# A float32 result tile for VectorE's top-k counts in a streaming hybrid encoder step

## The chip, the cores and the metric

The kernel runs on one core of one Trainium2 chip. The metric is the device time of one execution in microseconds. Three runs of the kernel before took 1585.16, 1585.86 and 1586.07 us; the median is 1585.86 us.

## The reference

One layer of an encoder works on 1024 new prompt frames and on 8 running streams of 16 frames, 1152 rows in all, each of 1024 features. After an RMSNorm a projection feeds two groups of heads side by side: a gated linear recurrence (the LRU: convolution over 4 frames, two gates, a scan) and sparse attention. An output projection and a SwiGLU feed-forward (2816 wide) with residuals close the layer. The part that matters here is how the attention chooses its keys:

```python
idx_score = einsum('bths,bth->bts', relu(sc), wi)          # one score per query and key
idx_score = where(adm, idx_score, -inf)                    # chunk-causal
vals, sel = lax.top_k(idx_score, topk)                     # 256 keys (prompt), 132 (streams)
```

For each query only the 256 (132) best keys take part in the softmax. The kernel doesn't sort: it finds each query's threshold bit by bit, and turns the scores into a mask of zeros and large negative numbers.

## The kernel before, in words

The rows are nine tiles of 128 queries: tiles 0 to 7 are the prompt, tile 8 (`NP`) the streams. Tiles 0 and 1 need no choice. The stages run after one another, with overlap: norm and the key and value projection, index scores, the LRU, the q projection, half of the output projection, attention, the other half, the feed-forward. All large products are matrix multiplications in three passes on split float32 (`mm3`; each pass is issued at line 205).

The threshold search runs in two groups (`TK`, read in `topk`). The group of tiles 2 to 5 counts on ScalarE: `activation(..., Sign, accum_out=cnt)`, 32 rounds of four counts. The group of tiles 6, 7 and 8 counts on VectorE: 16 rounds on the high 16 bits of the scores, a step (`topk_lower`) that makes a 16-bit key of what is left, and 16 more rounds, with three counts to a round (896, 1024 and 528 elements wide). A count is a `tensor_scalar` with `is_ge` whose elementwise result nobody reads; only the sum in `accum_out` is used. The result went to `jk[0]`, a bfloat16 tile that later stages use as well: `topk_lower` for a temporary, `topk_mask` for its equality mask, `sample_prep` for a copy of the last mask. After each round two or three tiny VectorE instructions (3 or 4 elements wide) update the candidate threshold (`cand`, `t`), for both groups: a ScalarE count of the next round waits for VectorE too.

Two planners set the order of the work. The first is the kernel's own: `run` steps generators (streams of work and `side` work) along an estimated clock, and `Metered` prices each instruction as it is issued. A VectorE instruction with `accum_out` and a 16-bit input is priced at 0.07 us plus half of 0.00104 us an element; the input's type decides, the result's type isn't looked at. That planner fixes the order in which the program is written down. The second is the scheduler of `TileContext(nc, schedule_with_timeline_sim=True)`: from the written order as priority, the dependencies and its own estimate of each instruction's time it sets the order in which each engine's queue finally holds its instructions. Within `step`, the top-k's instructions get a priority 400 places later than where they are written (`LATER`), so that they give way to others and fill gaps:

```python
    LATER = {'vector': 400, 'scalar': 400}
        with self.tc.high_priority(offset=-n):
            return next(g, None)
```

On the chip each engine's queue then runs strictly in that order. Instructions of one engine that the profile names by line 66 are all those recorded by `Metered`, so the tiles tell them apart: `jk` and `key` are the counts, `tk_cand` and `tk_cnt` the candidate updates, `xp`, `xc`, `tr`, `ti`, `tt` the LRU, `qn` and `rp` the queries, `acc` the output projection.

The LRU stage (`lru_main`): the matrix products of a third go to PSUM, ScalarE copies them out (`xp`), TensorE does the convolution on the copy (line 210), ScalarE adds the bias (`xc`), TensorE does the two gates, ScalarE and VectorE the rest.

Of the kernel before, what the change touches and what calls it, by code (L numbers as in the profile page):

```python
# [9 lines left out]
F32 = mybir.dt.float32  # L10
# [71 lines left out]
class Kernel:  # L82
# [181 lines left out]
    def build(self, upto=99):  # L264
        ctx, tc, nc, I, O = self.ctx, self.tc, self.nc, self.I, self.O
# [34 lines left out]
        with tc.tile_pool(name="t1a", bufs=2, side=R) as tp:  # L300
            g, wk = self.load_kv_weights(tp)
# [4 lines left out]
        groups = self.groups = [self.tk_group(n, t, a) for n, (t, a) in enumerate(self.TK)]  # L306
        widest = [max([2] + [s.shape[1] for i, s in self.s.items() for n, b in self.TK if i in n and a == b]) for a in range(2)]
        self.jk = [(tka_p if a else self.tk_p).tile([128, widest[a]], BF16, name=f"jk{a}") for a in range(2)]
        self.scored, self.masked, self.tk_done = set(), {0, 1}, set()
        self.qst, self.qst_t = {}, {}  # L310
        self.n_lru, self.spare = 0, None
# [531 lines left out]
    def topk_count(self, g, t, less=False):  # L843

        nc = self.nc
        for j, i in enumerate(g["tiles"]):
            w = self.s[i].shape[1]
            if g["act"]:
                nc.scalar.activation(self.jk[1][:, :w], self.s[i], AF.Sign, bias=t[:, j:j + 1],
                                     accum_out=g["cnt"][:, j:j + 1])  # L850
                continue
            k = 132 if i == NP else 256
            nc.vector.tensor_scalar(self.jk[0][:, :w], g["keys"][j], t[:, j:j + 1], 0.5 - k if less else None,
                                    op0=ALU.is_ge, op1=ALU.add, accum_out=g["cnt"][:, j:j + 1])
            if j % 2 and j + 1 < g["n"]:
                yield 0.0
# [893 lines left out]
```

## Time and profile before

| what | value |
|---|---|
| three runs, median | 1585.86 us |
| the profiled execution, its own time | 1582.82 us |
| its span in the profile | 1580.7 us |
| TensorE clock granted, mean | 0.969 |
| VectorE, ScalarE, GpSimd instructions | 1909, 1484, 433 |

The profile is of one execution. Its span is the time from the first to the last recorded instruction; the 2.1 us around it are in the execution's own time. Busy time of an engine is the time in which it works on an instruction; it doesn't count the time in which its queue's first instruction waits. An arrow `x <- y` between engines reads "waited for", one between tiles "written from".

### The profile page before, as it was taken

To read this page: it belongs to the slowest core of one execution; us is meant where nothing else is said; L and a number is where in the kernel's file an instruction comes from. 1 tells how busy PE (TensorE), PEld (TensorE's weight loads), DVE (VectorE), ACT (ScalarE), POOL (GpSimd) and SP (SyncE) were. 2 spreads that over 40 slices of the span, in tenths; PEclk is the share of its full clock that TensorE was granted. 3 is DMA by queue.
4 is the path that set the end of the run, shared out by engine and by line. 5 is a ranking of instruction groups with operands and counts; after the bars stand their busy time and mean duration, and the time that the engine had idled before them with its cause. 6 is when DMAs were issued, how large, how long until landed. Compare 5 with 4: busy or idle time off the path is not lost.

```text
span 1580.7 us, 21030 instructions
## 1 busy us (share of the span) xinstructions
PE 1477.3 (93%) x7858; PEld 1335.3 (84%) x7858; DVE 886.4 (56%) x1909; ACT 624.4 (39%) x1484; POOL 288.7 (18%) x433
## 2 busy tenths in 40 slices
PE   6899898875989899999999999999999999999998
PEld 6777676764977688888999999999898989898987
DVE  7656899998676887768424242423333242424143
ACT  5447967867631987755312120202020202121100
POOL 5424223227484444400000000000000000000000
PEclk7999899988999899999999999999999999999999
DMA  7211110100140001120302020202020202111002
GB/s 241 66 32 42 35 29 16 29 14 14 44 156 0 8 14 47 48 67 28 94 14 67 14 75 6 80 1 80 1 80 0 81 18 63 30 51 52 29 1 120
DMA packets 93798, 74.66 MB, mean 47 GB/s; under 512 B 13236, under 2 KB 84532, under 8 KB 93696
## 3 DMA queue, kind: packets, MB, share of 16 engines
q1 hardware_dynamic: 93696, 73.32, 15.5%
q8 instruction: 62, 1.02, 0.3%
q14 instruction: 40, 0.33, 0.1%
HBM read 67.03 MB, written 6.27 MB: 46 GB/s over the span
## 4 chain that ended last, share of the span: by engine, by line
PE 72%; DVE 15%; ACT 5%; POOL 3%; issue 3%; DMA 1%; SPq 0%; POOLq 0%; ACTq 0%; DVEq 0%
PE ps L205 67%; DVE jk L66 7%; PE ps L215 3%; DVE tk_cand L66 2%; ACT jk L66 1%; DVE tr L66 1%; POOL rp L66 1%; PE ps L210 1%; DVE ti L66 1%; POOL qn L66 1%; DVE s L66 1%; ACT qeo L66 1%; ACT m L66 1%; ACT relu L66 0%; DMA tab<-in_rope_dram 0%
## 5 line engine op out<-in xcount | busy, mean ns | idle before, releaser
L205 PE MATMUL ps<-hf,w 128*128 128x384 f32 x2556 | 460.6, 338 | 0.0
L205 PEld LDWEIGHTS ps<-hf,w 128*128 128x128 f32 x2556 | 451.5, 187 | 0.8
L205 PE MATMUL ps<-w,a 128*128 128x512 f32 x999 | 239.1, 390 | 0.0
L66 DVE TENSOR_TENSOR acc<-ps,acc 128x512 f32<-128x512 f32 x234 | 161.3, 690 | 134.4 <-PE ps L205 133.9
L205 PEld LDWEIGHTS ps<-w,a 128*128 128x128 f32 x999 | 187.3, 188 | 40.1
L66 ACT ACTIVATE w<-raw 128x512 fp32r<-128x512 f32 x128 | 77.8, 630 | 303.0 <-PE ps L205 220.9
L66 DVE TENSOR_TENSOR sg<-ps,sg 128x384 f32<-128x384 f32 x66 | 36.7, 557 | 276.4 <-PE ps L205 275.9
L66 DVE TENSOR_TENSOR w<-raw,w 128x512 fp32r<-128x512 f32 x116 | 76.8, 687 | 87.4 <-ACT w L66 87.2
L66 ACT ACTIVATE jk<-s,tk_cand 128x384 bf16<-128x384 f32 (+3 forms) x128 | 99.4, 776 | 61.8 <-DVE tk_cand L66 53.0
L66 ACT ACTIVATE a<-sg 128x384 fp32r<-128x384 f32 x66 | 34.5, 523 | 217.9 <-DVE sg L66 217.9
L205 PE MATMUL ps<-hf,rest 128*128 128x384 f32 x612 | 114.5, 334 | 0.0
L205 PE MATMUL ps<-h,w 128*128 128x384 f32 x576 | 108.7, 347 | 0.5 <-ACT relu L66 0.5
L205 PEld LDWEIGHTS ps<-hf,rest 128*128 128x128 f32 x612 | 106.9, 188 | 0.2
L205 PEld LDWEIGHTS ps<-h,w 128*128 128x128 f32 x576 | 102.3, 190 | 4.7 <-ACT relu L66 0.6
L205 PE MATMUL ps<-w,h 128*128 128x256 f32 (+1 forms) x600 | 94.6, 314 | 0.6 <-DVE to L66 0.6
L205 PE MATMUL ps<-w,rest 128*128 128x512 f32 x324 | 83.0, 406 | 8.2 <-POOL rest L66 8.0
L205 PEld LDWEIGHTS ps<-w,h 128*128 128x128 f32 x600 | 82.2, 188 | 7.3 <-DVE to L66 0.9
L205 PEld LDWEIGHTS ps<-w,rest 128*128 128x128 f32 x324 | 61.3, 194 | 22.7 <-POOL rest L66 8.9
L66 ACT ACTIVATE sg<-ps 128x384 f32<-128x384 f32 x66 | 32.1, 486 | 122.0 <-PE ps L205 122.0
L210 PE MATMUL ps<-xp,taps 128*128 128x384 f32 (+2 forms) x128 | 44.5, 504 | 37.7 <-ACT xp L66 37.7
L210 PEld LDWEIGHTS ps<-xp,taps 128*128 128x128 f32 x128 | 26.7, 231 | 51.7 <-issue 43.8
L66 POOL TENSOR_SCALAR m<-m,mx 128x128 f32<-128x128 f32 (+7 forms) x64 | 47.6, 752 | 68.5 <-DVE mx L66 61.7
(261 smaller groups left out, 2185.2 us busy)
## 6 DMA issues: line engine op xcount, KB each, us to landing
raw<-in_w_ffn_in_dram SPq DMA_DIRECT2D x44, 512.0 KB, 4.9
raw<-in_w_ffn_out_dram SPq DMA_DIRECT2D x22, 512.0 KB, 3.5
raw<-in_w_in_dram SPq DMA_DIRECT2D x16, 512.0 KB, 3.8
out_dram<-acc SPq DMA_DIRECT2D x9, 512.0 KB, 2.6
x<-in_x_prompt_dram SPq DMA_DIRECT2D x8, 512.0 KB
acc<-in_x_prompt_dram SPq DMA_DIRECT2D x8, 512.0 KB, 9.1
tab<-in_rope_dram SPq DMA_DIRECT2D x34, 64.0 KB, 1.8
raw<-in_w_out_dram SPq DMA_DIRECT2D x4, 512.0 KB, 3.5
```

Of the source, the lines that this page charges most:

```text
L66: return f(*args, **kw)
L205: self.nc.tensor.matmul(out, lhsT, rhs, start=start, stop=stop)
L210: self.nc.tensor.matmul(out, lhsT, rhs, start=start, stop=stop)
L215: self.nc.tensor.transpose(out, in_, self.ident[0:n, 0:n])
```

## The change

The counts of the VectorE group write their unused elementwise result to a tile of their own, `junk`, of float32, 1024 wide. `jk[0]` stays for its other uses. Nothing else is edited: the inputs, the operation, the sum and the number of instructions are the same. The new tile takes 4 KB of each partition.

```diff
         self.jk = [(tka_p if a else self.tk_p).tile([128, widest[a]], BF16, name=f"jk{a}") for a in range(2)]
+        self.junk = self.tk_p.tile([128, widest[0]], F32, name="junk")
 ...
             k = 132 if i == NP else 256
-            nc.vector.tensor_scalar(self.jk[0][:, :w], g["keys"][j], t[:, j:j + 1], 0.5 - k if less else None,
+            nc.vector.tensor_scalar(self.junk[:, :w], g["keys"][j], t[:, j:j + 1], 0.5 - k if less else None,
                                     op0=ALU.is_ge, op1=ALU.add, accum_out=g["cnt"][:, j:j + 1])
```

## Rows read from the trace of the kernel before

**Rows 1.** First part of the page: busy time, share, instructions of each engine.
```profile
PE 1477.3 (93%) x7858; PEld 1335.3 (84%) x7858; DVE 886.4 (56%) x1909; ACT 624.4 (39%) x1484; POOL 288.7 (18%) x433
```
**Rows 2.** Busy time by stretch; columns: from:to, length, engines, clock, DMA share, GB/s.
```profile
180.00:262.00 82.00, 74.27 (x358) 64.88 (x357) 79.05 (x233) 64.62 (x143) 15.22 (x26) 0.94 0.09 22
180.00:412.00 232.00, 185.18 (x913) 159.04 (x912) 216.14 (x534) 168.63 (x354) 72.23 (x96) 0.92 0.07 20
412.00:500.00 88.00, 79.00 (x476) 69.74 (x475) 60.95 (x107) 33.86 (x193) 65.54 (x82) 0.94 0.27 90
500.00:560.00 60.00, 52.50 (x280) 43.88 (x279) 47.16 (x163) 45.94 (x123) 21.92 (x40) 0.91 0.02 5
700.00:1000.00 300.00, 299.84 (x1586) 278.69 (x1585) 132.95 (x239) 76.54 (x144) 0.00 (x0) 1.00 0.14 42
1000.00:1580.00 580.00, 576.28 (x3016) 540.47 (x3014) 201.79 (x319) 93.40 (x174) 0.00 (x0) 1.00 0.15 47
```
**Rows 3.** Waits of PE, then ACT, 180 to 412 us: total us, times, longest.
```profile
PE ps L210 <- ACT xp L66: 37.7, 9, 8.9
PE ps L210 <- ACT xc L66: 8.6, 3, 3.8
...
ACT jk L66 <- DVE tk_cand L66: 48.3, 18, 5.6
```
**Rows 4.** Timeline of PE, 262 to 412 us: start, length, what, [idle before].
```profile
294.48 1.56 PE L210 MATMUL ps<-xc,bd 128*128 128x384 f32 x4 [3.84 <-ACT xc L66]
...
340.57 3.52 PE L210 MATMUL ps<-xp,taps 128*128 128x256 f32 x8 [8.91 <-ACT xp L66]
370.77 4.64 PE L210 MATMUL ps<-xp,taps 128*128 128x384 f32 x8 [8.08 <-ACT xp L66]
388.64 3.38 PE L210 MATMUL ps<-xp,taps 128*128 128x256 f32 x8 [7.77 <-ACT xp L66]
```
**Rows 5.** Timeline of ACT around those waits of PE.
```profile
338.60 0.61 ACT L66 ACTIVATE jk<-s,tk_cand 128x384 bf16<-128x384 f32 x1 [2.45 <-DVE tk_cand L66]
...
340.06 0.53 ACT L66 ACTIVATE xp<-ps 128x256 f32<-128x256 f32 x2
...
363.25 0.61 ACT L66 ACTIVATE jk<-s,tk_cand 128x384 bf16<-128x384 f32 x1
...
370.15 0.47 ACT L66 ACTIVATE xp<-ps 128x384 f32<-128x384 f32 x1
...
386.67 0.61 ACT L66 ACTIVATE jk<-s,tk_cand 128x384 bf16<-128x384 f32 x1 [5.61 <-DVE tk_cand L66]
```
**Rows 6.** Timeline of DVE, 330 to 339 us.
```profile
330.89 1.15 DVE L66 TENSOR_SCALAR_CACHE_REDUCE jk<-key,tk_cnt 128x896 bf16<-128x896 int16 x1
...
334.61 1.15 DVE L66 TENSOR_SCALAR_CACHE_REDUCE jk<-key,tk_cnt 128x896 bf16<-128x896 int16 x1
...
338.16 0.16 DVE L66 SCALAR_TENSOR_TENSOR tk_cand<-tk_cnt 128x4 int32<-128x4 f32 x1
```
**Rows 7.** Costliest DVE groups by form, 180 to 412 us: busy us, mean ns.
```profile
L66 DVE TENSOR_SCALAR_CACHE_REDUCE jk<-key,tk_cand 128x1024 bf16<-128x1024 bf16 x16 | 20.4, 1276 | 0.2
L66 DVE TENSOR_SCALAR_CACHE_REDUCE jk<-key,tk_cand 128x896 bf16<-128x896 bf16 x16 | 18.2, 1138 | 0.0
L66 DVE TENSOR_SCALAR_CACHE_REDUCE jk<-key,tk_cand 128x528 bf16<-128x528 bf16 x16 | 12.2, 761 | 0.2
L66 DVE TENSOR_SCALAR_CACHE_REDUCE jk<-key,tk_cnt 128x1024 bf16<-128x1024 int16 x16 | 20.5, 1278 | 0.4
L66 DVE DVE_READ_ACCUMULATOR jk<-key,tk_cand 128x1 f32 x48 | 3.9, 82 | 0.0
L66 DVE TENSOR_SCALAR jk<-jk,tk_cand,tk_cnt 128x512 f32<-128x512 f32 x4 | 2.2, 538 | 0.1
L66 DVE TENSOR_SCALAR key<-jk 128x512 int16<-128x512 f32 x4 | 1.7, 420 | 0.1
```
**Rows 8.** Timeline of DVE: a sum that writes float32, and first use of a mask.
```profile
371.17 1.25 DVE L66 TENSOR_SCALAR_CACHE_REDUCE s<-s,tk_cnt 128x1024 f32<-128x1024 f32 x1
...
534.03 0.55 DVE L66 CUSTOM_DVE_ANT_0 m<-ps,s 128x384 f32<-128x384 f32 x1
```
**Rows 9.** Timeline of POOL: the first mask of ScalarE's group is finished.
```profile
462.50 0.57 POOL L66 TENSOR_SCALAR s<-s 128x384 f32<-128x384 f32 x1
```
**Rows 10.** Timeline of PE: first use of what follows the VectorE group's masks.
```profile
587.19 0.27 PE L205 MATMUL ps<-jk,key 128*128 128x264 bf16 x1
```
**Rows 11.** Timeline of DVE: the copy of the last mask.
```profile
392.72 0.43 DVE L66 CAST jk<-s 128x528 bf16<-128x528 f32 x1 [0.53 <-POOL s L66]
```

## Prediction

> **What bounds the kernel now.** I read the page's first part, then busy time by stretch, then the waits of the stretches that are not full. TensorE is busy 93% of the span [rows 1]. By stretch it is full from 700 us to the end (299.84 of 300, then 576.28 of 580), and nothing on VectorE can matter there. The holes lie earlier: in 180 to 412 us, the LRU stage and all 96 counts of VectorE, TensorE works 185.18 of 232 us, so 46.8 us are idle [rows 2]. The waits name the cause of nearly all of it: 37.7 us for ScalarE's copy `xp` and 8.6 us for `xc`, 46.3 us together [rows 3].
>
> Why is the copy late? The timelines show a queue blocked at its head. At 340.57 TensorE has been idle for 8.91 us; the copy it needs starts at 340.06, behind a ScalarE count that had itself waited 2.45 us, to 338.60, for a candidate update on VectorE [rows 4, 5]. That update runs at 338.16, behind VectorE's counts, which follow each other from 330.89 on [rows 6]. At 388.64 it is the same: 7.77 us of idle TensorE, a count that waited 5.61 us [rows 4, 5]. In 180 to 412 ScalarE stood still 48.3 us on such updates, 18 times, with LRU copies queued behind [rows 3]. VectorE is the full engine of that stretch: 216.14 of 232 us [rows 2]. So the stage is paced by VectorE, through ScalarE's order, and TensorE pays.
>
> The sizes say what the scheduler may have got wrong. A round of three counts takes 1.276 + 1.138 + 0.761 us and three accumulator reads of 0.082, 3.42 us [rows 7]; one round's first count starts 3.72 us after the last one's (330.89 to 334.61) [rows 6]. The kernel's own meter prices the three at 3 x 0.07 + 2448 x 0.00052 = 1.48 us. A planner that believes that puts a ScalarE count early in ScalarE's queue, sure that its candidate will be there, and ahead of LRU copies; on the chip the candidate isn't there.
>
> **The change part by part.**
>
> *The duration of the 96 counts.* No row has this form with a 16-bit input and a float32 result. The nearest is the sum that reads and writes float32: 1.25 us at 1024 elements, against 1.276 for the count now [rows 7, 8]. That is below by 0.026 us: 96 x 0.026 = 2.5 us of VectorE less at the most. From above, the only rows in which a wider result goes with a longer time are two plain operations of the same width, 0.538 us to float32 and 0.420 us to int16 [rows 7]: a ratio of 1.28, though they differ in their scalar operands too. On the counts' busy time, that of the three groups with the 16-bit float key and as much again for the three with the integer key (whose 1024-wide group has 20.5 us against 20.4), 2 x (20.4 + 18.2 + 12.2) = 101.6 us [rows 7], that would be +28 us. I take 0, since the row with a sum is the nearest by far; the 28 us stay as a rival.
>
> The Trainium skill ("VectorE: DVE Perf Modes", section on the perf-mode tier table) speaks against the change here: it puts `tensor_scalar` at 4x for bfloat16 in SBUF and 2x for float32, so a wider result would drop the counts a tier. The plain operations' rows fit its 2x (0.538 us for 512 elements), the counts don't fit its 4x: 1024 elements in 1.276 us is less than one element a cycle at the page's 0.96 GHz. By the page as it stands the counts would get slower; by the row there is no faster mode to lose. The trace doesn't bear the page out for counts.
>
> *The extra tile.* It takes room, no instruction and no wait. The counts share their result tile with nobody else now; but all users of `jk[0]` around the counts are on VectorE too, one queue, so no wait goes: 0.
>
> *The kernel's own planner.* It prices by the input's type, which stays 16-bit. The written order and the due times don't move: 0.
>
> *The scheduler's order.* This is the whole effect. Its price for a count isn't in the profile, before or after. From both sides: nothing (it priced them alike) up to all of the 46.3 us of TensorE's waits [rows 3]; and a loss, below. To choose, I assume that it prices as the meter would: half rate for 16-bit throughout, full rate once a float32 is in it. A round is then believed to take 3 x 0.07 + 2448 x 0.00104 = 2.76 us instead of 1.48, against 3.42 on the chip: the error falls from 1.94 to 0.66 us a round, by 66%. A scheduler that sees VectorE busy sees the candidates come late, and puts ScalarE's LRU copies ahead of the counts that wait for them. 0.66 x 46.3 = 31 us. Not all of that can come: at 370.77 TensorE's 8.08 us were lost though the count at 363.25 hadn't waited for a candidate at all; the copy was behind four counts' own work and other LRU instructions [rows 4, 5]. I take off a third and keep 20 us.
>
> *What is late next.* VectorE's work doesn't shrink. In a stage shortened to 212 us, at the 96% that VectorE reached at its densest (79.05 of 82 us, 180 to 262) [rows 2], it does 204 of its 216 us; 12 us move behind the LRU, to 412 to 500, where VectorE has 88 - 60.95 = 27 us idle [rows 2] but also carries the query rotation and the output projection's sums. I charge half, 6 us. The masks have room: the VectorE group's last mask is copied at 392.72 and first used at 587.19 [rows 10, 11], 194 us; the first mask of ScalarE's group is ready at 463.07 and used at 534.03 [rows 8, 9], 71 us. If that cover is gone each further microsecond costs one.
>
> *Sum.* 1582.8 (the profiled execution) + 0 + 0 - 20 + 6 = 1568.8 us. The runs' median is 3.0 us above the profiled execution (1585.86 against 1582.82), so I say 1572 us.
>
> **The rivals.**
>
> *1. The order changes and the time doesn't.* For: VectorE is 93% busy in the stage whatever the order, so a copy freed early may meet an LRU instruction held on VectorE. Or the scheduler priced both forms alike, and the queues stay as they are. Against: ScalarE's 48.3 us of standing still are head-of-queue waits, and such waits depend on order alone. Time: 1583 to 1589.
>
> *2. The counts go too late (slower).* If the scheduler now holds VectorE's counts back behind everything it can find, rounds land after 412 us, in front of VectorE's sums and query work, which TensorE and GpSimd need. A round is 3.72 us; behind 412 there are 27 us idle to 500 and 12.8 to 560 [rows 2, 6], 40 in all. It decides from the point where the rounds moved exceed the idle time plus the gain: (40 + 20)/3.72, 16 of 32 rounds. At 19 rounds: 71 - 40 - 20 = +11, so about 1597. For: the top-k's instructions rank 400 places back, and every believed microsecond more makes them lose more contests. Against: they rank as far back now, and fill what is idle; the stage offers few other instructions to VectorE.
>
> *3. The chip pays for the wider result.* +28 us on an engine that paces its stage, of which the better order may give back some: 28 - 14 = +14, 1600. Against it stands the row with a sum into float32.
>
> **How the numbers follow.** A run can tell about 0.2% (3.2 us) from no change. Forecast (faster, own range 1555 to 1582): 0.60. Rival 1: 0.14. Rival 2: 0.22. Rival 3: 0.04. So faster 0.60, same 0.14, slower 0.26. The range must leave out no more than 2 in 10. The low end takes most of the order's 46.3 us with little given back: 1585.9 - 36 = 1550, about 5% left out below. The high end takes in rival 2 to its 19 rounds, 1597, and leaves out its worse half and most of rival 3: about 13%.
>
> **What would show it.** Right: counts of 1.28 us at 1024 in the profile after; in the LRU stage fewer waits of ScalarE's counts for `tk_cand` (48 us now) and of TensorE for `xp` (38 us now), the last LRU convolution earlier than 388 us by 15 to 20 us, and part of VectorE's counts or masks after it. The stages from attention on start earlier by about 14 us and have the same length. Wrong: counts near 1.6 us (rival 3); the same waits at the same places (rival 1); waits of TensorE for VectorE's `acc` or of GpSimd for `qn` in the 100 us after the LRU, or attention's first masked score waiting for a mask (rival 2).

## The result and the profile after

The kernel after takes 1565.93 us (median of 4 runs, 1565.71 to 1566.31) against 1585.96 us for the kernel before on the same chip: a ratio of 0.9877, 95% interval 0.9861 to 0.9892. The profiled execution took 1565.71 us, its span is 1563.9 us.

The first part of its page, beside [rows 1]:

```profile
PE 1472.8 (94%) x7858; PEld 1332.3 (85%) x7858; DVE 887.8 (57%) x1909; ACT 624.8 (40%) x1484; POOL 290.1 (19%) x433
```

Same instructions, nearly the same busy time on every engine. TensorE's busy time fell by 4.5 us, the span by 16.8: what went is mostly idle time of TensorE. To find where, I cut both traces at the start of the LRU's last convolutions on `xp` (393.14 us before, 362.53 after) and at the matrix product that first uses the VectorE group's masks [rows 10], which now starts at 571.39 us. Busy time by stretch (columns as in rows 2), the kernel before and then after:

```profile
0.00:180.00 180.00, 149.95 (x759) 126.67 (x760) 121.58 (x266) 107.28 (x268) 76.55 (x156) 0.91 0.30 88
180.00:393.14 213.14, 167.58 (x772) 142.16 (x771) 204.29 (x505) 156.05 (x331) 68.98 (x90) 0.91 0.08 22
393.14:587.19 194.05, 175.37 (x1048) 152.90 (x1047) 142.74 (x367) 113.97 (x383) 100.46 (x138) 0.95 0.13 44
587.19:1580.70 993.51, 984.44 (x5283) 913.59 (x5282) 417.80 (x774) 247.06 (x505) 42.68 (x50) 1.00 0.15 46
```
```profile
0.00:180.00 180.00, 149.03 (x750) 125.85 (x751) 120.61 (x262) 105.41 (x263) 76.14 (x156) 0.91 0.30 88
180.00:362.53 182.53, 162.92 (x780) 140.84 (x780) 168.18 (x447) 154.67 (x328) 56.00 (x84) 0.94 0.09 25
362.53:571.39 208.86, 177.78 (x1048) 153.25 (x1047) 181.10 (x427) 117.81 (x392) 115.37 (x144) 0.93 0.12 41
571.39:1563.90 992.51, 983.10 (x5283) 912.30 (x5282) 417.87 (x774) 246.91 (x505) 42.57 (x50) 1.00 0.15 46
```

The LRU stage is 30.6 us shorter, the stretch behind it 14.8 us longer, the rest 1.0 us shorter: together 16.8. Of the 30.6 us, 26.0 are idle time of TensorE (45.6 to 19.6), and 4.7 are busy time, at a mean granted clock of 0.94 instead of 0.91; of the 14.8 us, 12.4 are idle time (18.7 to 31.1). The fifth figure of each row (VectorE's busy time) says how: VectorE does 36.1 us less ahead of the LRU's end (204.29 to 168.18) and 38.4 us more behind it (142.74 to 181.10). ScalarE's work ahead of it hardly changes (156.05 to 154.67). Work of VectorE was put off, and the LRU went past it.

The waits that answer to [rows 3], the kernel after, TensorE and then ScalarE, 180 to 412 us:

```profile
PE ps L210 <- ACT xp L66: 18.4, 5, 5.7
...
PE ps L210 <- ACT xc L66: 0.7, 1, 0.7
```
```profile
ACT jk L66 <- DVE tk_cand L66: 21.0, 10, 4.6
```

TensorE's waits for the two copies fall from 46.3 us to 19.1, ScalarE's for the candidate from 48.3 to 21.0. The counts themselves, by form (busy us, mean ns), beside [rows 7]:

```profile
L66 DVE TENSOR_SCALAR_CACHE_REDUCE junk<-key,tk_cnt 128x1024 f32<-128x1024 int16 x16 | 20.4, 1274 | 0.1
L66 DVE TENSOR_SCALAR_CACHE_REDUCE junk<-key,tk_cand 128x1024 f32<-128x1024 bf16 x16 | 20.4, 1274 | 0.2
L66 DVE TENSOR_SCALAR_CACHE_REDUCE junk<-key,tk_cnt 128x896 f32<-128x896 int16 x16 | 18.2, 1140 | 0.3
...
L66 DVE TENSOR_SCALAR_CACHE_REDUCE junk<-key,tk_cand 128x528 f32<-128x528 bf16 x16 | 12.1, 756 | 0.0
```

1274 ns against 1276 for 1024 elements: the wider result costs nothing.

What was put off is best seen at the LRU's scans on VectorE. The LRU runs in four passes; the first scan of each pass, before and then after (timelines of VectorE; start, length):

```profile
265.04 0.95 DVE L66 TENSOR_TENSOR_SCAN tr<-tt,ti 128x384 f32<-128x384 f32 x1
...
317.99 0.95 DVE L66 TENSOR_TENSOR_SCAN tr<-tt,ti 128x384 f32<-128x384 f32 x1
...
374.12 0.94 DVE L66 TENSOR_TENSOR_SCAN tr<-tt,ti 128x384 f32<-128x384 f32 x1
...
409.45 0.95 DVE L66 TENSOR_TENSOR_SCAN tr<-tt,ti 128x384 f32<-128x384 f32 x1
```
```profile
255.54 0.95 DVE L66 TENSOR_TENSOR_SCAN tr<-tt,ti 128x384 f32<-128x384 f32 x1
...
297.93 0.95 DVE L66 TENSOR_TENSOR_SCAN tr<-tt,ti 128x384 f32<-128x384 f32 x1
...
340.23 0.95 DVE L66 TENSOR_TENSOR_SCAN tr<-tt,ti 128x384 f32<-128x384 f32 x1
...
378.48 0.95 DVE L66 TENSOR_TENSOR_SCAN tr<-tt,ti 128x384 f32<-128x384 f32 x1
```

From scan to scan the passes took 53.0, 56.1 and 35.3 us; now 42.4, 42.3 and 38.3. Counting along each engine's queue gives the reason (an engine runs its queue strictly in order, as the forced orders below show too, so this needs no times):

```
                                                      pass 1   2    3    4
VectorE counts ahead of the pass's first scan, before     48   72   96   96   (of 96)
                                               after      36   50   72   90
ScalarE counts ahead of the pass's last xp copy, before   48   72   98  118   (of 128)
                                                 after    48   68   92  113
```

In VectorE's queue the LRU overtakes 12, 22, 24 and 6 counts. At the 3.42 us of a round of three that is 13.7, 25.1, 27.4 and 6.8 us of VectorE's work that no longer stands ahead of the scans. In ScalarE's queue only up to six counts change sides. The last count now starts at 398.26 us (352.70 before), and the three scans that build VectorE's masks, which ran from 355.02 to 384.33, now run from 405.35 to 433.33.

### The profile page after: what moved, and what is told of

It is laid out like the page before. It is cut to its first block, busy times and chain, and to the rows that moved or that the text cites. A ratio compares the mean times of both kernels' runs of the same rounds, so it can differ in the third digit from the quotient of the medians.

```text
span 1563.9 us, 21015 instructions
## 1 busy us (share of the span) xinstructions
PE 1472.8 (94%) x7858; PEld 1332.3 (85%) x7858; DVE 887.8 (57%) x1909; ACT 624.8 (40%) x1484; POOL 290.1 (19%) x433
## 4 chain that ended last, share of the span: by engine, by line
PE 74%; DVE 10%; ACT 9%; issue 3%; POOL 3%; DMA 1%; SPq 0%; POOLq 0%; ACTq 0%; DVEq 0%
PE ps L205 69%; ACT jk L66 4%; PE ps L215 4%; DVE junk L66 2%; PE ps L210 1%; DVE tk_cand L66 1%; ACT L66 1%; POOL rp L66 1%; DVE tr L66 1%; DVE jk L66 1%; DVE ti L66 1%; ACT qeo L66 1%; ACT tr L66 1%; DVE qn L66 1%; DVE s L66 1%
## 5 line engine op out<-in xcount | busy, mean ns | idle before, releaser
L66 ACT ACTIVATE jk<-s,tk_cand 128x384 bf16<-128x384 f32 (+3 forms) x128 | 99.4, 777 | 31.3 <-DVE tk_cand L66 25.8
L210 PE MATMUL ps<-xp,taps 128*128 128x384 f32 (+2 forms) x128 | 40.1, 466 | 19.1 <-ACT xp L66 18.4
L205 PE MATMUL ps<-smr,vhl 128*128 128x512 f32 x162 | 53.8, 418 | 2.7 <-ACT smr L66 2.7
```

The costliest lines, as they stand in the source:

```text
L66: return f(*args, **kw)
L205: self.nc.tensor.matmul(out, lhsT, rhs, start=start, stop=stop)
L210: self.nc.tensor.matmul(out, lhsT, rhs, start=start, stop=stop)
```

## The experiments

Ratios are to the kernel before on the same chip, with 95% intervals. Where nothing else is said, waits are TensorE's for `xp` and `xc` in 180 to 412 us.

**Room or type.** The first run keeps bfloat16 in a tile of its own; the second has the float32 result but lets the tile double as `jk[0]`, so it has no room of its own.

```diff
-        self.junk = self.tk_p.tile([128, widest[0]], F32, name="junk")         # first run
+        self.junk = self.tk_p.tile([128, 2 * widest[0]], BF16, name="junk")   # first run
 ...
+        self.jk[0] = self.junk.bitcast(BF16)                                  # second run, with the F32 tile
```

> The counts get room of their own, 4 KB of a partition as in the change, but the result stays bfloat16. Theory (the scheduler's longer estimate of a float32 result makes the order): as before, 1583 to 1589 us, with about 46 us of TensorE's waits for xp and xc in the LRU stage; the queues do differ a little, since the first count after topk_lower no longer has to follow its temporaries in jk[0]. Rival (the own room takes away a dependency, and that is what pays): 1563 to 1570 us, waits for xp and xc near 19 us.

> No room of its own: the counts write a float32 tile that also serves as jk[0] for topk_lower, the masks and the mask copy. Theory (estimate): 1563 to 1572 us, last LRU convolution near 363 us instead of 394. Rival (room): as before, 1583 to 1589 us. Rival (any new order of the queues moves the time by some 1% at random): e1 and e2 lie anywhere, unrelated to the type.

The own room alone: 1583.83 us, 0.9986 [0.9977, 0.9995], waits 46.4 us. The float32 alone: 1560.20 us, 0.9835 [0.9821, 0.9850], waits 16.7 us. The second is 2.8 us under my range. So the type carries the gain. VectorE's counts ahead of the four first scans say the same: 48, 74, 96 and 96 in the first run, 36, 50, 72 and 89 in the second. The first run and the kernel after differ in nothing but the type of that tile, which takes the same room. The scheduler's price itself stands in no record; that it believes a count with a float32 result to be longer is inferred from this difference and from the counts going later.

The room alone has no fixed sign: with bfloat16 it is worth 2 us, with float32 it costs 6 (0.9877 with it, 0.9835 without). Either way the scheduler orders some instructions of VectorE and ScalarE otherwise. With a tile of its own the first count behind `topk_lower` no longer has to follow that step's temporaries in `jk[0]`; that this is the reason was not tried by itself.

**Half a dose.** Float32 for the 16 high rounds alone, then for the 16 low rounds alone; the others write to `jk[0]` as before.

```diff
-            nc.vector.tensor_scalar(self.junk[:, :w], g["keys"][j], t[:, j:j + 1], ...
+            nc.vector.tensor_scalar((self.jk[0] if less else self.junk)[:, :w], ...   # high rounds
+            nc.vector.tensor_scalar((self.junk if less else self.jk[0])[:, :w], ...   # low rounds
```

> float32 result in own room for the 16 rounds on the high bits (from 182 us on), bfloat16 in jk[0] for the 16 rounds on the low key. Theory: the part of the 31 us that the LRU stage gained which falls before about 280 us comes, the rest does not: 1570 to 1580 us. Random-order rival: anywhere from 1560 to 1590. Own-room rival: as before.

> The reverse: bfloat16 in jk[0] for the high bits, float32 in own room for the low key (from 282 us on). Theory: most of TensorE's waits before (39 of 46 us) lie after 262 us, so this half brings more than e3: 1566 to 1576 us, below e3. Own-room rival: nearly all of the gain, 1563 to 1570, with e3 as before.

High: 1568.40 us, 0.9889 [0.9873, 0.9906], waits 28.4 us. Low: 1575.78 us, 0.9938 [0.9923, 0.9952], waits 31.3 us. Each half gives a part and the waits fall with it. The first is 1.6 us under my range, and I had the halves the wrong way round: the early rounds are worth more. The first scans show where. With the high rounds alone the first two passes stand where they stand in the kernel after (256.13 and 298.34 us) and the third slips to 351.42; with the low rounds alone the first starts at 267.16, 11.6 us later than in the kernel after, and the others, at 314.38, 355.69 and 399.41, are 15 to 21 us later.

**Is it ScalarE's wait for the candidate?** ScalarE's counts get a constant threshold and count tiles of their own, so they never wait for VectorE's updates; this leaves out the choice of keys for tiles 2 to 5 (one tiny VectorE instruction is added behind the rounds). Once on the kernel before, once on the kernel after; the edit's main lines:

```diff
-                nc.scalar.activation(self.jk[1][:, :w], self.s[i], AF.Sign, bias=t[:, j:j + 1],
+                nc.scalar.activation(self.jk[1][:, :w], self.s[i], AF.Sign, bias=self.b0,
...
+            if g["act"]:
+                g["cnt"] = self.cnts[31 - b]
```

> The kernel before, but ScalarE's counts take a constant for their threshold and write each round's sums to a tile of their own, so that none of them waits for VectorE (the choice of keys of tiles 2 to 5 is left out; the counts and VectorE's updates all still run). Theory (TensorE's waits come from ScalarE's queue standing still in front of a count that waits for a candidate update): ScalarE's 48 us of waits for tk_cand go, TensorE's waits for xp and xc fall from 46 us to under 20, the time to 1555 to 1572 us. Rival (the LRU's own instructions on VectorE are late behind the counts, and that is what held the stage): waits and time stay near those of before, above 1578 us.

> The same edit on the changed kernel (float32 result). Theory: with nothing on ScalarE waiting for VectorE the type has little left to mend: within 8 us of x1_bf16_noupd, against the 20 us between the two kernels without this edit. Rival (VectorE's own queue): still 15 us or more below x1_bf16_noupd.

Before: 1580.64 us, 0.9965 [0.9953, 0.9978]. After: 1553.12 us, 0.9796 [0.9781, 0.9811]. The theory that I argued in the prediction fails here. If ScalarE's standing still for `tk_cand` were the root, its removal should have brought the kernel before close to the kernel after; it brought 5 us, and the distance between the two grew from 20 to 27.5. The waits of ScalarE in the first of the two, 180 to 412 us:

```profile
ACT L66 <- DVE tr L66: 20.7, 2, 12.5
ACT tr L66 <- DVE tr L66: 17.3, 2, 8.7
```

The 48.3 us for `tk_cand` are gone and 38.0 us for the LRU's own `tr` have come. TensorE's waits, in the first run and then in the second:

```profile
PE ps L210 <- ACT xp L66: 39.5, 6, 14.2
...
PE ps L210 <- ACT xc L66: 0.7, 1, 0.7
```
```profile
PE ps L210 <- ACT xp L66: 11.4, 6, 4.4
...
PE ps L210 <- ACT xc L66: 0.7, 1, 0.7
```

The 5 us are not the worth of the removed wait alone, because the scheduler ordered the queues anew: as nothing holds ScalarE's counts back, more of them stand ahead of the passes' last `xp` copies (54, 84, 116 and 128 in the first run, against 48, 72, 98 and 118 in the kernel before). But the two runs of the pair are alike in this: the second has 55, 85, 116 and 128. They differ in VectorE's queue, where 48, 75, 96 and 96 counts stand ahead of the four first scans in the first run and 35, 50, 71 and 83 in the second, and they lie 27.5 us apart. I read it so: ScalarE's queue meets the lateness of VectorE's at whatever instruction depends on it next; the candidate was only the first such instruction.

**The other planner, and the masks held back.** In the first run the kernel's own planner prices counts of a 16-bit input at the full rate; in the second the VectorE group's threshold and masks are not written down until the attention's keys are done. Both start from the kernel after.

```diff
-            ... kw.get("accum_out") is not None and args[1].dtype in (BF16, I16):
+            ... kw.get("accum_out") is not None and args[1].dtype in (BF16, I16) and False:
```
```diff
+        while not g["act"] and not self.k_done:
+            yield 1.0
         self.topk_threshold(g)
```

> The changed kernel, with the kernel's own planner also pricing a count with a 16-bit input at the full rate (0.00104 us an element instead of half). Theory (the gain is a better estimate): the first planner's estimate gets better too, but the scheduler had already mended most of the order: 1558 to 1568 us. Rival (any believed delay of the counts helps): clearly below 1558. Rival (any new order moves the time at random): outside 1550 to 1575 either way.

> The changed kernel, with the masks of VectorE's group (scans, comparisons, 25 us of VectorE) held back until the keys are rotated, near the end of the first output half. In the changed kernel they run from 405 to 440 us, amid the query rotation, and TensorE waits 18.4 us there for the split rest, 8.0 before. Theory (what the change gave back, it gave back to those masks): the waits for rest fall to about 8 us and the time by 8 to 14 us, to 1552 to 1558 us. Rival (the query stage can't be shorter once the LRU stage ends early; its own chain of GpSimd work sets it): 1562 to 1568 us. Other rival: the masks are late for attention, above 1570 us.

1560.20 us, 0.9842 [0.9828, 0.9857], waits 16.3 us; and 1562.63 us, 0.9855 [0.9841, 0.9870], waits 14.1 us. The first planner under-prices the counts too, and telling it so is worth another 5 to 6 us on this kernel. The second run doesn't test what it was made for: the scans that build the masks still ran from 401 to 429 us, so being written later did not make them late. It stays inconclusive on the give-back.

**The order by itself.** Here the type and the order are taken apart. The first run counts in bfloat16, but each queue is tied to the order of the kernel after: a first pass with the float32 tile finds it, a second lays it down as edges between neighbours of one queue, which issue nothing and wait for nothing. The second run counts in float32 in the order of the kernel before. The edit, shortened:

```diff
+    for forced in (False, True):
 ...
+                hymba_step(tc, I, O, forced)     # the tile's type depends on the pass
+                for x in order:                  # the first pass's order, engine by engine
+                    tc.add_manual_dep(x, last[x.engine], NoSync)
```

> The counts write bfloat16 in a tile of their own, but every engine's queue is forced into exactly the order that the kernel after has (the order is found in a first pass with the float32 tile and laid down as issue order in a second). Theory (the order is everything, the type on the chip nothing): 1566 us, 1562 to 1570, TensorE's waits for xp and xc in 180 to 412 us 16 to 23 us. Rival (float32 is itself cheaper on the chip, the order brings little): 1580 to 1586, with waits of 40 us and more.

> The counts write float32 in a tile of their own, but every engine's queue is forced into exactly the order that the kernel before has. Theory (order alone): 1586 us, 1582 to 1589, TensorE's waits for xp and xc 42 to 50 us, the count of 1024 elements 1.28 us. Rival (the type itself gains on the chip): 1562 to 1570.

1565.10 us, 0.9865 [0.9851, 0.9880], with waits of 19.4 us, where the kernel after has 1565.93 and 19.1. And 1585.52 us, 0.9995 [0.9986, 1.0004], with 47.1 us, where the kernel before has 1585.96 and 46.3. In both traces the instructions of TensorE, VectorE, ScalarE and GpSimd follow one another, by operation and tiles, exactly as in the trace whose order they were given. TensorE's waits, the bfloat16 run and then the float32 run:

```profile
PE ps L210 <- ACT xp L66: 18.4, 5, 5.7
...
PE ps L210 <- ACT xc L66: 1.0, 1, 1.0
```
```profile
PE ps L210 <- ACT xp L66: 42.2, 10, 9.0
PE ps L210 <- ACT xc L66: 4.9, 3, 2.2
```

The counts of the float32 run:

```profile
L66 DVE TENSOR_SCALAR_CACHE_REDUCE junk<-key,tk_cnt 128x1024 f32<-128x1024 int16 x16 | 20.5, 1278 | 0.4
L66 DVE TENSOR_SCALAR_CACHE_REDUCE junk<-key,tk_cand 128x1024 f32<-128x1024 bf16 x16 | 20.4, 1277 | 0.2
```

That settles it: the order gives the time, whichever type is written; the type gives nothing, whichever order it stands in. Which engine's queue carries it was not tried by itself. The queue counts above speak for VectorE's, and so does the pair without ScalarE's waits, in which ScalarE's counts stand alike and VectorE's don't.

**Where 15 us are given back.** In the kernel after TensorE waits for GpSimd's `rest` in the q projection. Its waits from 380 to 570 us, and the longest of them:

```profile
PE ps L205 <- POOL rest L66: 18.4, 5, 10.9
...
PE ps L205 <- DVE qeo L66: 3.0, 1, 3.0
...
PE ps L215 <- POOL m L66: 0.5, 1, 0.5
```
```profile
443.40 2.93 PE L205 MATMUL ps<-w,rest 128*128 128x512 f32 x6 [10.94 <-POOL rest L66]
```

GpSimd's timeline up to that point: the mask steps (`s`) and the rotations (`rp`) stand ahead of the `rest` that TensorE needs:

```profile
429.67 2.14 POOL L66 TENSOR_TENSOR s<-s,jk 128x1024 f32<-128x1024 f32 x1
431.77 3.21 POOL L66 TENSOR_TENSOR rp<-qn,tab 128x128 f32<-128x128 f32 x4
...
435.19 1.04 POOL L66 TENSOR_SCALAR s<-s 128x1024 f32<-128x1024 f32 x1
438.79 1.16 POOL L66 TENSOR_TENSOR rp<-qn,tab 128x128 f32<-128x128 f32 x2 [2.56 <-DVE tail L66]
439.92 1.37 POOL L66 TENSOR_TENSOR s<-s,jk 128x384 f32<-128x384 f32 x1
441.25 0.86 POOL L66 TENSOR_TENSOR rp<-qn,tab 128x128 f32<-128x128 f32 x2
442.07 1.28 POOL L66 TENSOR_TENSOR rest<-yF,rest 128x512 fp32r<-128x512 f32 x1
```

Before, that wait was 8.0 us in all; its growth by 10.4 us makes up most of the 12.4 us that TensorE idles more in this stretch. So the next run pushes the VectorE group's masks out of this stage (they are also written down only when the attention begins):

```diff
+            self.last_acc = nc.vector.tensor_tensor(a, po, a, op=ALU.add)
 ...
+        held = lambda: ExitStack() if x is None else self.tc.issue_after(x)   # x: the last acc of the first half
+            with held():
                 self.topk_mask(g, j)
```

> The kernel after, with VectorE's threshold and mask instructions of tiles 6 to 8 held in its queue behind the last sum (acc) of the output projection's first half. Theory (what is given back behind the LRU is given back to those masks): TensorE's waits for GpSimd's rest in 380 to 500 us fall from 18 to 8 to 11 us, time 1553 to 1560. Rival 1 (the q stage is bound by GpSimd's rest for other reasons, the masks only happen to lie there): those waits stay at 16 to 20 us, time 1562 to 1569. Rival 2 (the masks now come late for attention): TensorE or GpSimd wait for masks after 560 us, time over 1570.

1561.68 us, 0.9845 [0.9830, 0.9859]: beside the first theory's range (1553 to 1560) and just under the first rival's (1562 to 1569). Its waits of TensorE, 400 to 570 us:

```profile
PE ps L205 <- POOL rest L66: 9.3, 2, 5.7
PE ps L215 <- POOL m L66: 7.9, 8, 2.4
PE ps L205 <- DVE qeo L66: 7.4, 3, 4.1
```

The wait for `rest` halves, as the first theory said, but TensorE now waits for masked scores and for `qeo` in the attention instead: 9.1 us less here, 11.8 us more there. The stretch from the LRU's last convolutions to the first use of the masks takes 210.68 us, against 208.86 in the kernel after; the 4 us that the run gains lie in its LRU stage (175.33 us against 182.53), which the new order changed as well. So the masks' place in the q projection is not by itself what costs. The stretch is 15 us longer than before with the masks early in it and 17 us longer with them late. Only the masks were moved, not the 17 counts that run behind the LRU's last copy as well; what those cost by themselves, and whether a third place is cheaper, is not shown.

**Shared room and full price together.** The float32 tile that shares its room with `jk[0]`, and the full price in the kernel's own planner.

> The float32 result tile shares its room with jk[0], and the kernel's own planner prices a count of 16-bit input at the full 0.00104 us an element. Theory (each of the two alone gave 1560.2; both tell a planner that VectorE is busier than it believed, so they gain from the same waits): no sum of gains, 1556 to 1562. Rival (the gains are of different waits and add): 1551 to 1556. Rival (two prices corrected overshoot and VectorE's rounds land behind the LRU): 1563 to 1572.

1561.31 us, 0.9837 [0.9820, 0.9853], waits 16.3 us: no sum of gains. From the kernel after, the shared room alone and the full price alone each reach 1560.20 us, and the intervals of the three runs overlap. The run with the full price alone has both planners' prices raised already; on the kernel that counts in bfloat16 the full price was not tried.

## Why the prediction was right, and where not

- **The counts' duration: 0.** Right, 1274 ns against 1276, and float32 in the forced order ran as long as the kernel before. By the perf-mode tier table of the Trainium skill ("VectorE: DVE Perf Modes") a wider result would have cost some time here; it cost none, 1274 ns against 1276. Another page agrees with the trace: the Trainium skill ("SBUF — State Buffer", section "Who interferes with whom") leaves the form of `tensor_scalar` that writes out its accumulator out of the two-port modes. One reading beside the 0 doesn't hold: the plain operation at 0.538 us does 512 elements at 952 a us, also fewer than the one a cycle that the prediction holds against the counts; only the one at 0.420 us does more. The 0 doesn't rest on it.
- **The extra tile: 0.** Not quite: no wait went, but the order changed with it. The room is worth 2 us with bfloat16 and costs 6 with float32, which is what the change has.
- **The kernel's own planner: 0.** Right for this change. Its price, when it is corrected, is worth 5 to 6 us where the float32 tile has its own room (0.9842 against 0.9877) and nothing where it shares that of `jk[0]` (0.9837 against 0.9835).
- **The scheduler's order: -20 us.** The step was right that the type moves the order and that TensorE's 46.3 us of waits are what there is to gain. Its size was too small: the waits fell by 27 us and the LRU stage by 30.6. The price that the 66% rest on stands in no record, so that its 31 us come close to the 30.6 is no evidence for it. A third was too much to take off, but the reason for it held: the copy whose lateness cost 8.08 us at 370.77 costs 5.71 in the kernel after, behind ScalarE's own work again, and that is the longest wait left:

```profile
342.32 4.40 PE L210 MATMUL ps<-xp,taps 128*128 128x384 f32 x8 [5.71 <-ACT xp L66]
```

- **The mechanism within that step** was wrong in the queue. I had ScalarE's LRU copies moving ahead of ScalarE's counts; up to six counts moved there. In VectorE's queue up to 24 did. What I described as rival 2 (VectorE's rounds held back behind the LRU) is what happened, with 17 of 96 counts behind the last copy, some six rounds, far below the 16 from which I said it costs more than it gives.
- **What is late next: +6 us.** The kind was right and the size not: 14.8 us. I counted 12 us of moved work and charged half; 38 us moved. This miss of 9 us and the one of 11 us in the gain point opposite ways; that the net came out within 3.1 us is luck.
- **The 3.0 us** between the profiled execution and the median don't belong to the kernel: after, they are 0.2. Of the 6.1 us by which 1572 is too high, 3.1 are the net of order and give-back (17.1 instead of 14) and 2.8 are this; the rest is rounding.
- Of what should show it: the waits, the counts and the part of VectorE's work behind the LRU came as said; the last LRU convolutions came 31 us earlier, not 15 to 20; the stages behind kept their length (992.51 us against 993.51).

## What to carry to other kernels

Where a scheduler orders the queues by its own estimate of durations, a wrong price on an engine that is full can cost time at the engines that depend on it, and the type of an operand that nobody reads can set the order. Look for it by comparing a chain's believed time with its time in the trace, and then count in the queues what stands ahead of the critical stage on each engine, before you blame the wait that the profile shows at the end of the chain. Work put off from one stage is paid for in part in the next one: count the whole of it.

## What the runs showed of the hardware

The result's type is free in a count: 1274 to 1278 ns for 1024 elements, with a bfloat16 or float32 result and a bfloat16 or int16 input.

In the stretch behind the LRU a VectorE product of two SBUF operands took six times as long beside a GpSimd product as with GpSimd idle. Two of one form in the kernel after, the first beside GpSimd's `s<-s,jk` of 429.67 to 431.81 us (shown above), the second while GpSimd stood idle, from 436.23 to 438.79:

```profile
429.74 2.35 DVE L66 TENSOR_TENSOR qn<-qn,tab 128x256 f32<-128x256 f32 x1 [0.35 <-POOL rp L66]
...
437.85 0.40 DVE L66 TENSOR_TENSOR qn<-qn,tab 128x256 f32<-128x256 f32 x1
```

2.35 us against 0.40, and the slow one ends 0.28 us behind GpSimd's instruction. The Trainium skill ("SBUF — State Buffer", section "Who interferes with whom") says that such a VectorE instruction contends with a GpSimd one that reads SBUF, and calls their shared pair of ports an exclusive lock. This pair of rows agrees; it is one pair, not a trial. How much of the 14.8 us it makes was not tried.
